# The modulation products of the second layer as VectorE multiply-adds into PSUM, TensorE summing over partitions

## Chip, cores and metric

The kernel runs on one core of a Trainium2 chip. The metric is device time of one execution, in microseconds (us), lower being better. Before the change the median of three runs was 3017.8 us (3013.01 to 3021.67).

## The reference

The reference is a two-layer diffusion backbone on 1024 latent tokens and 256 context tokens, width 1024. Layer 0 mixes tokens by retention and gated linear attention, layer 1 by windowed attention; each layer ends with a squared-ReLU MLP of width 4096. Every sub-layer is modulated by six vectors that come from one product per layer with a vector `c` (for latent tokens) or `c_ctx` (for context tokens). That product is what the change concerns:

```python
def modulation(cvec, w, b):
    m = jax.nn.silu(cvec) @ w + b          # (1024,) @ (1024, 6144) + (6144,)
    return jnp.split(m[..., None, :], 6, axis=-1)

sh1, sc1, g1, sh2, sc2, g2 = modulation(c, w_mod[i], b_mod[i])
csh1, csc1, cg1, csh2, csc2, cg2 = modulation(c_ctx, w_mod[i], b_mod[i])
h = x * (1.0 + sc1) + sh1
x = sublayer_residual(x, y, g1, ...)       # layer_norm(alpha * x + gate * y)
x = sublayer_residual(x, sq_relu_mlp(x * (1.0 + sc2) + sh2, mlp_w1[i], mlp_w2[i]), g2, ...)
```

In layer 1, the last one, the context tokens end after the keys and values of the attention, so that of the `c_ctx` vectors only `csh1` and `csc1` are used there. `w_mod[1]` is 1024 x 6144 in fp32, 24 MB. Nothing in layer 1 reads its modulation before the MLP of layer 0 is done.

## The kernel before

Activations lie with the channel on the partitions: a tile `acc` of [128, 8, N] holds 1024 channels of N tokens. There are three chunks of tokens, `CH`: chunk 0 (the context, N = 256) and chunks 1 and 2 (N = 512 each). Every product with a weight is done in three matmuls, high part by high, high by low and low by high (`mm3`, lines 200, 201, 202), since fp32r rounds. `wsplit` (lines 183 to 190) loads 128 x 1024 of a weight (line 185, SyncE's queue), rounds it on ScalarE (line 188) and makes the rest on GpSimd (line 189).

The change acts in the MLP of layer 0 (`mlp(0, ...)`). It runs over 16 blocks `b` of 256 hidden channels, and in each over the chunks 0, 1, 2; in the first and last block the chunks of 512 are cut in two halves, so that all steps there have N = 256. A step does `up` (2 x 8 x 3 matmuls into the PSUM banks 2 and 3), then ScalarE and VectorE square the result and split it (lines 981 to 985), and then `down` of the step before (8 output groups `m` of 6 matmuls each, into a ring of the four banks 0, 1, 4, 5). VectorE adds each group to `acc` (line 999), which frees its bank. So the order on TensorE is up of step n, down of step n-1, up of step n+1, and so on.

The modulation of layer 1 is worked off inside this MLP, by a generator `fill` that is advanced three times per step: after `up`, after group `m` = 3 and after group `m` = 7 of `down`. The generator is `mod_steps(1, s, mp, 1, 512)` for s = 0, 1, 2. Each advance consumes one tile `raw` of 128 x 512 of `w_mod[1]` (one of 96, one buffer, loaded at line 111 on SyncE's queue) with four matmuls (line 114): `cs`, which is SiLU of the two vectors in columns 0 and 1 and zeros up to 32, is the stationary operand, and each quarter of `raw` streams through another group of 32 columns of the array, so that the results of four quarters stand on four groups of 32 partitions of PSUM bank 7. An fp32 matmul is two records in the trace. After 32 loads `mt` is copied to SBUF by ScalarE (line 117), turned by four transposes (line 120), and VectorE adds the bias and writes `mod`, `osc` and `gta` (lines 127 to 133).

A scheduler orders each engine's instructions when the program is built; at run time every engine takes its own in that order. SyncE's queue (SP) carries the loads of the MLP's weights and of `raw`, in one order.

Of the kernel before, what the change touches and what calls it, by code (L numbers as in the profile page):

```python
# [34 lines left out]
def backbone(ctx: ExitStack, tc: tile.TileContext, xT, cin, wmod, bmod, lng, lnb, w1, w2,  # L35
# [9 lines left out]
    V, S, G, TE, SY = nc.vector, nc.scalar, nc.gpsimd, nc.tensor, nc.sync  # L45

    cp = ctx.enter_context(pool(name="cp", bufs=1))
    cp.tile([P, 16], F32, tag="pad", name="pad")
    edge = ctx.enter_context(pool(name="edge", bufs=1, side="right"))
    edge.tile([P, 120], F32, tag="edge", name="edge")  # L50
    rawp = ctx.enter_context(pool(name="rawp", bufs=3))
# [5 lines left out]
    def nm(s):  # L57
        uid[0] += 1
        return f"{s}_{uid[0]}"
# [27 lines left out]
    G.memset(ones_d, 1.0 / 1024.0)  # L87
    ones_1 = const([32], "ones_1")
    G.memset(ones_1, 1.0 / 32.0)
    ones_h = const([32], "ones_h")  # L90
    G.memset(ones_h, 1.0 / 128.0)
    eps_t = const([1], "eps_t")
# [9 lines left out]
    def mod_steps(l, s, mdp, nb=1, w=1024, tags=("raw",), bank=None):  # L102

        pM_ = bank or pM
        pt = pM_()
        n_ = 0
        for o in range(0, 2048, w):
            for k in range(KT):
                raw = mdp.tile([P, w], F32, tag=tags[n_ % len(tags)], name=nm("raw"), bufs=nb)
                n_ += 1  # L110
                SY.dma_start(raw, wmod[l, k * P:(k + 1) * P, s * 2048 + o:s * 2048 + o + w])
                yield
                for g in range(4):
                    TE.matmul(pt[32 * g:32 * g + 32, o // 4:(o + w) // 4], lhsT=cs[:, k, :],
                              rhs=raw[:, g * w // 4:(g + 1) * w // 4], start=(k == 0), stop=(k == KT - 1))
        mt = mdp.tile([P, w], F32, tag=tags[0], name=nm("mt"), bufs=nb)[:, 0:512]
        S.copy(mt, pt)
        p2 = pM_()
        for q in range(4):
            TE.transpose(p2[:, q * P:(q + 1) * P], mt[:, q * P:(q + 1) * P], ident)  # L120
        vw = "p (q g i) -> p g q i" if w == 1024 else "p (q g i) -> p q g i"
        fw = "p (g q) -> p g q" if w == 1024 else "p (q g) -> p q g"
        pv = p2.rearrange(vw, q=4, g=4)
        for si in range(2):
            idx = 2 * s + si
            sub = pv[:, :, 2 * si:2 * si + 2, 0:2] if w == 1024 else pv[:, 2 * si:2 * si + 2, :, 0:2]
            V.tensor_tensor(
                mod[:, l, idx, :, :].rearrange(fw.replace(") ->", ") j ->") + " j", g=4), sub,
                bm[:, l, idx, :].rearrange(fw, g=4)[:, :, :, None].to_broadcast(list(sub.shape)), ALU.add)
            if idx in (1, 4):  # L130
                V.tensor_scalar(osc[:, l, idx // 3], mod[:, l, idx], 1.0, None, op0=ALU.add)
            if idx in (2, 5):
                V.tensor_scalar(gta[:, l, idx // 3], mod[:, l, idx], 1.0 / ALPHA, None, op0=ALU.mult)
        yield

    def mod_chunks(l, s, bank):

# [926 lines left out]
    with pool(name="m0", bufs=1) as mp:  # L1064
        ln_ = layer_norm_steps(accs[2][:, :, 256:512], 0, 0, mp, "ln_s", "ln_q", 1, True, pL, 512)
        early = Early([new_h(hp, 1, 0, hp, (0,), (V, V)) + new_h(hp, 1, 0, hp, (256,)) + new_h(hp, 2, 0, hp, (0,)), [(None, ln_)] + new_h(hp, 2, 0, hp, (256,))], ((2, 2), (2, 2)))
        early.need(1, 0)
        adv(ln_, 1)
        hn = {}

        ticks0, ticks1 = (4, 1), (3, 2)
        norms, hgens = [], []

        def tick(k, to_free=False):
            k, kh = k
            while norms and (k > 0 or to_free):
                r_ = next(norms[0][0], "end")
                if r_ == "end":
                    hgens.append(norms.pop(0)[1])
                k -= 1  # L1080
                if k <= 0 and r_ in ("end", "free"):
                    break
            while hgens and kh > 0:
                if next(hgens[0], "end") == "end":
                    hgens.pop(0)
                else:
                    kh -= 1

        def post(ci, o0, n):
            norms.append((post_norm(accs[ci][:, :, o0:o0 + n]), post_h(ci, o0, n)))  # L1090

        def post_norm(acc):
            yield from layer_norm_steps(acc, 0, 1, (rawp, hp), "raw", "hf", 1, True, pL, 512)

        def post_h(ci, o0, n):
            sl = slice(o0, o0 + n)
            if ci > 0:
                SY.dma_start(xd[ci][:, :, sl], accs[ci][:, :, sl])
            if stop == "x2":
                SY.dma_start(dbg[:, :, CH[ci][0] + o0:CH[ci][0] + o0 + n], accs[ci][:, :, sl])  # L1100
            if o0 == 0:
                hn[ci] = h_tiles(hp, ci)
            yield from h_steps(accs[ci][:, :, sl], 1, 0, cj(ci), hn[ci][0][:, :, sl], hn[ci][1][:, :, sl], hp, "hf", 2, S)

        rest = mlp(0, [0, 1, 2], hs, accs, wg, mp, post, chain(*[mod_steps(1, s_, mp, 1, 512) for s_ in range(3)]), tick, ticks0, early)
        tick((1, 0), True)
        hs = hn

# [415 lines left out]
```

## Time and profile before

| | us |
|---|---|
| median of three runs | 3017.8 (3013.01 to 3021.67) |
| the profiled execution's own time | 3027.1 |
| its span, first to last instruction | 3025.3 |
| TensorE busy in the span | 2922.6 (97%) |
| VectorE busy | 1525.4 (50%) |
| ScalarE busy | 976.4 (32%) |
| GpSimd busy | 809.9 (27%) |

Durations below are of the one profiled execution, which took 9.3 us more than the median of the runs. Of its 3027.1 us, 1.8 lie outside the span. PE is TensorE, PEld its weight loads, DVE is VectorE, ACT ScalarE, POOL GpSimd, SP SyncE. Matmuls are pipelined: a record is longer than the time by which it moves the next one back, so what a matmul costs is read from start to start, not from its length.

### The profile page before, as it was taken

The numbers are of one execution on the slowest core, as the hardware profiler recorded it, in microseconds if no ns is written. First come the engines' busy times: TensorE is split into PE (matmuls) and PEld (weight loads), VectorE is DVE, ScalarE is ACT, GpSimd is POOL, SyncE is SP. The second block draws the span as 40 slices with busy tenths as digits, with TensorE's granted clock in tenths as the row PEclk, the third lists the DMA queues.
The fourth block names the chain that finished last, engine by engine and source line by source line (L and its number), as shares of the span: only waits on it lengthen the run. The fifth ranks groups of instructions, "written<-read, shape, count | busy, mean of one in ns | idle before, by whom it ended". The sixth has DMA issues, their size and how long they took to land. (4 is left out here: it accounts for less than half of the span.)

```text
span 3025.3 us, 43318 instructions
## 1 busy us (share of the span) xinstructions
PE 2922.6 (97%) x17856; PEld 2386.6 (79%) x17856; DVE 1525.4 (50%) x2489; ACT 976.4 (32%) x1617; POOL 809.9 (27%) x609
## 2 busy tenths in 40 slices
PE   7989998999999999999999999999999999999997
PEld 4766788888888888888888777677678888888886
DVE  3654477777434333433334654666775333333445
ACT  4534344444211111111111442556653221112113
POOL 3120145445211111111111342244344221122121
PEclk9999999999999999999999999999999999999999
DMA  7278575663222222221100166222221111111111
GB/s 254 96 229 254 185 260 193 202 202 112 78 70 79 68 80 67 80 67 49 42 29 15 67 200 179 75 79 74 71 70 63 56 56 36 49 56 50 36 41 56
DMA packets 164261, 304.52 MB, mean 101 GB/s; under 512 B 13504, under 2 KB 90560, under 8 KB 163552
## 3 DMA queue, kind: packets, MB, share of 16 engines
q1 hardware_dynamic: 145648, 272.91, 28.0%
q0 software_dynamic: 6480, 16.26, 1.9%
q10 hardware_dynamic: 11936, 12.59, 1.4%
q8 instruction: 140, 2.29, 0.3%
q14 instruction: 57, 0.47, 0.0%
HBM read 257.67 MB, written 44.04 MB: 100 GB/s over the span
## 5 line engine op out<-in xcount | busy, mean ns | idle before, releaser
L189 POOL TENSOR_TENSOR w<-raw,w 128x1024 fp32r<-128x1024 f32 x210 | 507.4, 2424 | 1683.4 <-ACT w L188 1642.9
L999 DVE SCALAR_TENSOR_TENSOR acc<-k,gta,acc 128x512 f32<-128x512 f32 (+1 forms) x704 | 443.2, 648 | 831.0 <-PE k L202 823.7
L200 PE MATMUL k<-hh,w 128*128 128x256 f32 (+1 forms) x1632 | 556.9, 342 | 5.1 <-DVE hh L196 3.4
L201 PE MATMUL k<-hl,w 128*128 128x256 f32 (+1 forms) x1632 | 555.0, 340 | 4.0 <-POOL hl L197 3.4
L202 PE MATMUL k<-hh,w 128*128 128x256 f32 (+1 forms) x1632 | 551.1, 338 | 0.2 <-POOL w L189 0.2
L188 ACT CAST w<-raw 128x1024 fp32r<-128x1024 f32 x260 | 269.5, 1048 | 822.5 <-PE k L202 540.3
L200 PE MATMUL k<-uh,w 128*128 128x512 f32 (+1 forms) x1408 | 503.0, 357 | 4.2 <-DVE acc L999 4.0
L201 PE MATMUL k<-ul,w 128*128 128x512 f32 (+1 forms) x1408 | 495.4, 352 | 0.0
L202 PE MATMUL k<-uh,w 128*128 128x512 f32 (+1 forms) x1408 | 494.8, 351 | 0.0
L200 PEld LDWEIGHTS k<-hh,w 128*128 128x128 f32 x1632 | 312.5, 192 | 54.9 <-issue 16.3
L201 PEld LDWEIGHTS k<-hl,w 128*128 128x128 f32 x1632 | 312.5, 192 | 44.8 <-issue 7.6
L202 PEld LDWEIGHTS k<-hh,w 128*128 128x128 f32 x1632 | 312.4, 191 | 34.4 <-issue 2.8
L200 PEld LDWEIGHTS k<-uh,w 128*128 128x128 f32 x1408 | 266.5, 189 | 55.4 <-issue 14.2
L981 ACT ACTIVATE r<-k 128x512 f32<-128x512 f32 (+1 forms) x176 | 90.9, 516 | 649.7 <-PE k L202 649.0
L202 PEld LDWEIGHTS k<-uh,w 128*128 128x128 f32 x1408 | 266.7, 189 | 36.7 <-issue 1.0
L201 PEld LDWEIGHTS k<-ul,w 128*128 128x128 f32 x1408 | 266.7, 189 | 35.3 <-issue 0.8
L200 PE MATMUL k<-yh,w 128*128 128x256 f32 (+1 forms) x544 | 183.9, 338 | 10.1 <-DVE acc L693 10.1
L201 PE MATMUL k<-yl,w 128*128 128x256 f32 (+1 forms) x544 | 181.2, 333 | 0.0
L202 PE MATMUL k<-yh,w 128*128 128x256 f32 (+1 forms) x544 | 181.1, 333 | 0.0
L984 DVE TENSOR_TENSOR r<-r 128x1024 f32<-128x1024 f32 (+1 forms) x88 | 113.9, 1295 | 127.7 <-ACT uh L983 127.4
L673 POOL TENSOR_SCALAR acc<-acc,lg_t,lb_t 128x256 f32<-128x256 f32 x124 | 103.1, 847 | 116.1 <-DVE acc L667 46.8
L200 PEld LDWEIGHTS k<-yh,w 128*128 128x128 f32 x544 | 106.5, 196 | 22.6 <-DVE acc L693 11.5
(300 smaller groups left out, 4419.2 us busy)
## 6 DMA issues: line engine op xcount, KB each, us to landing
raw<-in_w SPq DMA_DIRECT2D x128, 512.0 KB, 3.4
raw<-in_wo SPq DMA_DIRECT2D x72, 512.0 KB, 3.5
raw<-in_wmod SPq DMA_DIRECT2D x128, 256.0 KB, 2.7
raw<-in_wfm SPq DMA_DIRECT2D x48, 512.0 KB, 5.6
raw<-in_wmod SPq DMA_DIRECT2D x32, 512.0 KB, 4.2
kt<-kd SPq DMA_DIRECT2D x20, 512.0 KB, 6.0
qt<-qT POOLq DMA_DIRECT2D x32, 256.0 KB, 4.3
qT<-qT ACTq DMA_DIRECT2D x30, 256.0 KB, 3.7
```

Of the source, the lines that this page charges most:

```text
L188: S.copy(hi, raw)
L189: (eng or G).tensor_tensor(lo, raw, hi.bitcast(F32), ALU.subtract)
L200: TE.matmul(pt, lhsT=wh, rhs=xh, start=start, stop=False)
L201: TE.matmul(pt, lhsT=wh, rhs=xl, start=False, stop=False)
L202: TE.matmul(pt, lhsT=wl, rhs=xh, start=False, stop=stop)
L673: G.tensor_scalar(acc[:, k, :], acc[:, k, :], lg_t[:, l, s, k:k + 1], lb_t[:, l, s, k:k + 1], op0=ALU.mult, op1=ALU.add)
L981: S.activation(rf[:, i, :n], pts[i][:, :n], AF.Relu)
L984: V.tensor_tensor(rf[:, :, :n], rf[:, :, :n], rf[:, :, :n], ALU.mult)
L999: V.scalar_tensor_tensor(a_, pt[:, :n], gta[:, l, 1, m, cj(ci):cj(ci) + 1], a_, op0=ALU.mult, op1=ALU.add)
```

## The change

The three calls of `mod_steps` for layer 1 are replaced by three of a new generator, `mod_sums`. It loads the same 96 times 256 KB of `w_mod[1]` into one buffer `raw`. The multiplications by SiLU of the vectors, and the sum over the eight blocks of 128 input channels, are now VectorE's: for the first block `pt = raw * cs[:, 0, j]`, for the others `pt = raw * cs[:, k, j] + pt`, with `pt` in PSUM bank 7. What is left of the sum, over the 128 partitions, is done by TensorE: `pt` is copied to SBUF by ScalarE and each 128 columns of it are the stationary operand of a matmul whose moving operand is one column of ones, `one_c`. The result is one column per 128 output channels, on the partitions where `mod` needs it, so there are no transposes.

For s = 0 (`sh1` and `sc1`) both vectors are needed: there the tile holds two blocks of 256 columns, and each load is followed by four VectorE instructions on 128 x 256. For s = 1 and 2 only the latent vector is computed, one instruction on 128 x 512 per load. In all there are 128 + 64 such instructions, 16 copies instead of 3, and 16 x 4 matmuls with one moving column in place of 384 matmuls with 128 and 12 transposes. The generator has 128 steps, before it had 99. The padding of the constants' pool is cut from 16 to 8 columns.

```diff
@@ -45,7 +45,7 @@
     V, S, G, TE, SY = nc.vector, nc.scalar, nc.gpsimd, nc.tensor, nc.sync
 
     cp = ctx.enter_context(pool(name="cp", bufs=1))
-    cp.tile([P, 16], F32, tag="pad", name="pad")
+    cp.tile([P, 8], F32, tag="pad", name="pad")
     edge = ctx.enter_context(pool(name="edge", bufs=1, side="right"))
     edge.tile([P, 120], F32, tag="edge", name="edge")
     rawp = ctx.enter_context(pool(name="rawp", bufs=3))
@@ -87,6 +87,8 @@
     G.memset(ones_d, 1.0 / 1024.0)
     ones_1 = const([32], "ones_1")
     G.memset(ones_1, 1.0 / 32.0)
+    one_c = const([1], "one_c")
+    G.memset(one_c, 1.0)
     ones_h = const([32], "ones_h")
     G.memset(ones_h, 1.0 / 128.0)
     eps_t = const([1], "eps_t")
@@ -132,6 +134,45 @@
             if idx in (2, 5):
                 V.tensor_scalar(gta[:, l, idx // 3], mod[:, l, idx], 1.0 / ALPHA, None, op0=ALU.mult)
         yield
+
+    def mod_sums(l, s, mdp, bank):
+
+
+        nj = 2 if s == 0 else 1
+        w = 512 // nj
+        nb = w // P
+        for o in range(0, 2048, w):
+            pt = bank()
+            for k in range(0, KT, nj):
+                raw = mdp.tile([P, 512], F32, tag="raw", name=nm("raw"), bufs=1)
+                SY.dma_start(raw.rearrange("p (a c) -> p a c", a=nj),
+                             wmod[l, k * P:(k + nj) * P, s * 2048 + o:s * 2048 + o + w]
+                             .rearrange("(a p) c -> p a c", p=P))
+                yield
+                for a in range(nj):
+                    src = raw[:, a * w:(a + 1) * w]
+                    for j in range(nj):
+                        dst = pt[:, j * w:(j + 1) * w]
+                        if k + a == 0:
+                            V.tensor_scalar(dst, src, cs[:, 0, j:j + 1], None, op0=ALU.mult)
+                        else:
+                            V.scalar_tensor_tensor(dst, src, cs[:, k + a, j:j + 1], dst, op0=ALU.mult, op1=ALU.add)
+            mt = mdp.tile([P, 512], F32, tag="raw", name=nm("mt"), bufs=1)
+            S.copy(mt, pt)
+            yield
+            p2 = bank()
+            for b in range(4):
+                TE.matmul(p2[:, b:b + 1], lhsT=mt[:, b * P:(b + 1) * P], rhs=one_c, start=True, stop=True)
+            idx = 2 * s + o // 1024
+            ks = slice(o % 1024 // P, o % 1024 // P + nb)
+            for j in range(nj):
+                V.tensor_tensor(mod[:, l, idx, ks, j], p2[:, j * nb:(j + 1) * nb], bm[:, l, idx, ks], ALU.add)
+                if idx in (1, 4):
+                    V.tensor_scalar(osc[:, l, idx // 3, ks, j], mod[:, l, idx, ks, j], 1.0, None, op0=ALU.add)
+                if idx in (2, 5):
+                    V.tensor_scalar(gta[:, l, idx // 3, ks, j], mod[:, l, idx, ks, j], 1.0 / ALPHA, None,
+                                    op0=ALU.mult)
+            yield
 
     def mod_chunks(l, s, bank):
 
@@ -1102,7 +1143,7 @@
                 hn[ci] = h_tiles(hp, ci)
             yield from h_steps(accs[ci][:, :, sl], 1, 0, cj(ci), hn[ci][0][:, :, sl], hn[ci][1][:, :, sl], hp, "hf", 2, S)
 
-        rest = mlp(0, [0, 1, 2], hs, accs, wg, mp, post, chain(*[mod_steps(1, s_, mp, 1, 512) for s_ in range(3)]), tick, ticks0, early)
+        rest = mlp(0, [0, 1, 2], hs, accs, wg, mp, post, chain(*[mod_sums(1, s_, mp, pM) for s_ in range(3)]), tick, ticks0, early)
         tick((1, 0), True)
         hs = hn
```

VectorE, in the first third of the stage, a `down` of chunk 0 with N = 256 (`acc_370` is chunk 0's accumulator, L999 before and L1040 after is the addition that frees a bank, L984/L985 and L1025/L1026 are the squaring and splitting of the step before). Before:

```order
L999 SCALAR_TENSOR_TENSOR acc_370_2834<-k_1050_7769,gta,acc_370_2834 128x256
L984 TENSOR_TENSOR r_7755<-r_7755 128x1024
L999 SCALAR_TENSOR_TENSOR acc_370_2834<-k_1051_7777,gta,acc_370_2834 128x256
L985 TENSOR_TENSOR ul_7756<-r_7755,uh_7759 128x1024
L999 SCALAR_TENSOR_TENSOR acc_370_2834<-k_1052_7785,gta,acc_370_2834 128x256
L999 SCALAR_TENSOR_TENSOR acc_370_2834<-k_1053_7793,gta,acc_370_2834 128x256
L999 SCALAR_TENSOR_TENSOR acc_370_2834<-k_1055_7807,gta,acc_370_2834 128x256
```

The same place after, with the two loads whose products come just ahead of it:

```order
L159 SCALAR_TENSOR_TENSOR k_1020_7539<-raw_7625,cs,k_1020_7539 128x256 x4
L159 SCALAR_TENSOR_TENSOR k_1020_7539<-raw_7662,cs,k_1020_7539 128x256 x4
L1040 SCALAR_TENSOR_TENSOR acc_370_2836<-k_1052_7767,gta,acc_370_2836 128x256
L1040 SCALAR_TENSOR_TENSOR acc_370_2836<-k_1053_7775,gta,acc_370_2836 128x256
L1025 TENSOR_TENSOR r_7753<-r_7753 128x1024
L159 SCALAR_TENSOR_TENSOR k_1020_7539<-raw_7700,cs,k_1020_7539 128x256
L1026 TENSOR_TENSOR ul_7754<-r_7753,uh_7757 128x1024
L159 SCALAR_TENSOR_TENSOR k_1020_7539<-raw_7700,cs,k_1020_7539 128x256
L1040 SCALAR_TENSOR_TENSOR acc_370_2836<-k_1054_7783,gta,acc_370_2836 128x256
L159 SCALAR_TENSOR_TENSOR k_1020_7539<-raw_7700,cs,k_1020_7539 128x256
L1040 SCALAR_TENSOR_TENSOR acc_370_2836<-k_1055_7791,gta,acc_370_2836 128x256
L159 SCALAR_TENSOR_TENSOR k_1020_7539<-raw_7700,cs,k_1020_7539 128x256
```

Four multiply-adds on 128 x 256 stand between the additions of this `down`, and eight ahead of it, each four of which need their own load of the one buffer.

VectorE, later, between a `down` of chunk 0 and the next of chunk 1, while TensorE does an `up`. Before, with nothing of the modulation there:

```order
L999 SCALAR_TENSOR_TENSOR acc_370_2834<-k_1171_8708,gta,acc_370_2834 128x256
L999 SCALAR_TENSOR_TENSOR acc_370_2834<-k_1172_8716,gta,acc_370_2834 128x256
L999 SCALAR_TENSOR_TENSOR acc_371_2836<-k_1180_8794,gta,acc_371_2836 128x512
L984 TENSOR_TENSOR r_8780<-r_8780 128x1024
L999 SCALAR_TENSOR_TENSOR acc_371_2836<-k_1181_8802,gta,acc_371_2836 128x512
```

After, a like place:

```order
L1040 SCALAR_TENSOR_TENSOR acc_370_2836<-k_1517_11228,gta,acc_370_2836 128x256
L1040 SCALAR_TENSOR_TENSOR acc_370_2836<-k_1518_11236,gta,acc_370_2836 128x256
L159 SCALAR_TENSOR_TENSOR k_1508_11174<-raw_11306,cs,k_1508_11174 128x512
L159 SCALAR_TENSOR_TENSOR k_1508_11174<-raw_11340,cs,k_1508_11174 128x512
L159 SCALAR_TENSOR_TENSOR k_1508_11174<-raw_11375,cs,k_1508_11174 128x512
L159 SCALAR_TENSOR_TENSOR k_1508_11174<-raw_11457,cs,k_1508_11174 128x512
L1040 SCALAR_TENSOR_TENSOR acc_371_2838<-k_1526_11308,gta,acc_371_2838 128x512
L1025 TENSOR_TENSOR r_11297<-r_11297 128x1024
```

Four multiply-adds with four loads stand in a row, ahead of the additions of the next `down`.

TensorE, between a `down` and an `up`. Before, the four matmuls of one load:

```order
L201 MATMUL k_1494_11221<-ul_10986,w_10270 128x512
L202 MATMUL k_1494_11221<-uh_10989,w_10270 128x512
L114 MATMUL k_1358_10191<-raw_11194,cs 32x128 x4
L200 MATMUL k_1496_11235<-hh_6751,w_10695 128x512
L201 MATMUL k_1496_11235<-hl_6752,w_10695 128x512
```

After, between two groups of a `down`, the four matmuls that sum one `mt` over its partitions:

```order
L242 MATMUL k_1096_8089<-ul_7892,w_6906 128x512
L243 MATMUL k_1096_8089<-uh_7895,w_6906 128x512
L165 MATMUL k_1097_8096<-one_c,mt_8063 128x1 x4
L241 MATMUL k_1098_8104<-uh_7895,w_6901 128x512
L242 MATMUL k_1098_8104<-ul_7892,w_6901 128x512
```

There are 96 places of the first kind before, and 16 of the second after.

## Rows read from the trace of the kernel before

**Rows 1.** Busy time of each engine in four stretches (stretch, its length, then busy us and, in brackets, instructions of PE, PEld, DVE, ACT and POOL; granted clock; share of the DMA engines; GB/s). The MLP of layer 0 runs from about 741 to 1640 us.

```profile
740.00:760.00 20.00, 19.56 (x148) 15.89 (x147) 18.15 (x29) 13.71 (x29) 13.17 (x11) 1.00 0.18 58
760.00:780.00 20.00, 19.87 (x176) 18.08 (x176) 16.10 (x28) 8.05 (x16) 11.74 (x12) 1.00 0.23 66
...
900.00:1000.00 100.00, 100.00 (x589) 80.78 (x588) 38.16 (x53) 17.15 (x24) 14.41 (x7) 1.00 0.22 67
741.00:1640.00 899.00, 895.09 (x5351) 744.87 (x5351) 353.57 (x516) 167.93 (x241) 163.01 (x81) 1.00 0.20 62
```

**Rows 2.** TensorE in order of time between an `up` and a `down` with N = 512 (start us, length us, engine, line, operation, tiles, shapes).

```profile
907.84 0.39 PE L202 MATMUL k<-hh,w 128*128 128x512 f32 x1
...
908.52 0.39 PE L202 MATMUL k<-hh,w 128*128 128x512 f32 x1
908.84 0.43 PE L114 MATMUL k<-raw,cs 128*32 128x128 f32 x8
909.20 0.50 PE L200 MATMUL k<-uh,w 128*128 128x512 f32 x1
909.53 0.39 PE L201 MATMUL k<-ul,w 128*128 128x512 f32 x1
```

**Rows 3.** The same in a `down` with N = 256.

```profile
953.68 0.28 PE L201 MATMUL k<-ul,w 128*128 128x256 f32 x1
953.80 0.28 PE L202 MATMUL k<-uh,w 128*128 128x256 f32 x1
954.01 0.43 PE L114 MATMUL k<-raw,cs 128*32 128x128 f32 x8
954.37 0.38 PE L200 MATMUL k<-uh,w 128*128 128x256 f32 x1
954.59 0.28 PE L201 MATMUL k<-ul,w 128*128 128x256 f32 x1
```

**Rows 4.** Groups of instructions on TensorE from 741 to 1640 us, shapes kept apart (line, engine, operation, tiles, shapes, count | busy us, mean ns | idle us just before them, and what ended it).

```profile
L114 PE MATMUL k<-raw,cs 128*32 128x128 f32 x768 | 41.3, 285 | 3.3 <-DMA raw<-in_wmod 3.3
...
L120 PE MATMUL k<-ident,mt 128*128 128x128 f32 x12 | 1.8, 273 | 0.0
```

**Rows 5.** TensorE around the transposes of one `mt`.

```profile
934.39 0.39 PE L200 MATMUL k<-uh,w 128*128 128x512 f32 x1
934.62 0.60 PE L120 MATMUL k<-ident,mt 128*128 128x128 f32 x4
934.97 0.47 PE L201 MATMUL k<-ul,w 128*128 128x512 f32 x1
935.28 0.39 PE L202 MATMUL k<-uh,w 128*128 128x512 f32 x1
```

**Rows 6.** TensorE in the scans of layer 0: two fp32 matmuls (four records) with 128 x 128 stationary and 64 moving columns.

```profile
396.81 0.56 PE L904 MATMUL k<-qt,S 128*128 128x64 f32 x4
397.21 0.44 PE L902 MATMUL k<-Pg,vt 128*128 128x128 f32 x2
```

**Rows 7.** Groups of instructions on VectorE from 750 to 1700 us, shapes kept apart, columns as in rows 4.

```profile
L999 DVE SCALAR_TENSOR_TENSOR acc<-k,gta,acc 128x512 f32<-128x512 f32 x224 | 165.5, 747 | 250.8 <-PE k L202 250.3
L999 DVE SCALAR_TENSOR_TENSOR acc<-k,gta,acc 128x256 f32<-128x256 f32 x182 | 82.1, 478 | 190.8 <-PE k L202 190.4
...
L649 DVE TENSOR_TENSOR acc<-acc,k 128x512 f32<-128x512 f32 x11 | 7.1, 676 | 0.0
```

**Rows 8.** VectorE in a `down` of chunk 0 (N = 256), in order of time; the last column is idle time and what ended it.

```profile
951.96 0.48 DVE L999 SCALAR_TENSOR_TENSOR acc<-k,gta,acc 128x256 f32<-128x256 f32 x1 [11.39 <-PE k L202]
952.41 1.23 DVE L984 TENSOR_TENSOR r<-r 128x1024 f32<-128x1024 f32 x1
953.56 0.48 DVE L999 SCALAR_TENSOR_TENSOR acc<-k,gta,acc 128x256 f32<-128x256 f32 x1
953.95 1.21 DVE L985 TENSOR_TENSOR ul<-r,uh 128x1024 fp32r<-128x1024 f32 x1
955.08 1.65 DVE L999 SCALAR_TENSOR_TENSOR acc<-k,gta,acc 128x256 f32<-128x256 f32 x4
957.05 0.48 DVE L999 SCALAR_TENSOR_TENSOR acc<-k,gta,acc 128x256 f32<-128x256 f32 x1 [0.32 <-PE k L202]
957.77 0.48 DVE L999 SCALAR_TENSOR_TENSOR acc<-k,gta,acc 128x256 f32<-128x256 f32 x1 [0.23 <-PE k L202]
```

**Rows 9.** The loads of `raw` at line 111 (those of layer 0 among them).

```profile
L111 SPq DMA_DIRECT2D raw<-in_wmod x112: 327/328/797, 185.6 to 1372.5; - x112
...
DMA to landing us min/median/max: 2.4/2.6/6.2
```

**Rows 10.** The loads at line 142, of two blocks of 128 x 512 of `w_mod[0]` in one (512 KB).

```profile
L142 SPq DMA_DIRECT2D raw<-in_wmod x16: 378/378/384, 395.7 to 656.8; - x16
...
DMA to landing us min/median/max: 3.5/4.1/6.7
```

**Rows 11.** VectorE in the first block of the MLP, the longest idle time before 785 us.

```profile
784.49 0.69 DVE L984 TENSOR_TENSOR r<-r 128x512 f32<-128x512 f32 x1 [5.46 <-ACT uh L983]
```

**Rows 12.** ScalarE's copies of `mt` before (four in all, one of them in layer 0).

```profile
L117 ACT COPY mt<-k x4: 586/590/591, 285.5 to 1377.0; 128x512 f32<-128x512 f32 x4
```

## Prediction

> **What bounds the kernel now.** I looked first at the busy times by stretch [rows 1], because the change touches one stage alone, the MLP of layer 0. There TensorE is busy for 895.09 of 899 us at a granted clock of 1.00 (the upper of its two levels, 2.4 GHz), and VectorE for 353.57, some 39%. A busy TensorE may still wait inside its records, so I looked next at what VectorE waits for [rows 7]: nearly all its idle time ahead of the additions of line 999 (250.3 of 250.8 us, 190.4 of 190.8) ended with a matmul. TensorE sets the pace, VectorE follows. So time taken off TensorE in this stage comes off the end, until VectorE is late. The reader should see one exception in the same view: from 740 to 780 us VectorE is busy for 18.15 and 16.10 of 20 us [rows 1], since the layer norms and splits of the first chunks lie there.
>
> **What is removed.** A matmul's cost is read from start to start. With N = 512 the starts are 0.227 us apart (907.84 to 908.52 for three). Around the eight records of one load it is 908.52 to 909.53 for two steps, 1.01 us; less 2 x 0.227 that is 0.556 us [rows 2]. With N = 256 the starts are 0.12 apart, and two steps with a load between take 953.80 to 954.59, 0.79 us; less 0.24 that is 0.55 [rows 3]. The two agree, though the matmuls around them differ by a factor of two, so I take 0.553 for each load. There are 768 records [rows 4], so 96 loads: 96 x 0.553 = 53.1 us. The three times four transposes cost 934.39 to 935.28 less 2 x 0.227, 0.44 us each [rows 5], 1.3 us together. TensorE also waited 3.3 us for loads of `raw` [rows 4]; VectorE will wait for them in its place. Removed in all: 57.7 us.
>
> **What is added on TensorE.** Sixteen times four fp32 matmuls, eight records, with 128 x 128 stationary and one moving column. No row has one moving column. The nearest has the same stationary shape and 64 columns: four records from 396.81 to 397.21, 0.10 us each [rows 6], so 0.80 us for eight and 12.8 us for sixteen. From above the transposes bound it, 0.11 per record [rows 5]: 14.1 us. From below the eight records with 32 stationary columns do, 0.55 [rows 2, 3]: 8.8 us. I take 12.8, by the row with the same stationary operand. A gain is excluded, since these matmuls replace nothing that is not counted already. Net on TensorE: 57.7 - 12.8 = 44.9 us.
>
> **What is added on VectorE.** On 128 x 256, multiply-adds that follow each other start 0.39 us apart (four in 1.65 us, one 0.48) [rows 8]; 128 of them are 50 us. On 128 x 512 the addition of line 999 has a mean of 0.747 and line 649 one of 0.676 [rows 7]; at 0.7, 64 are 45 us. None of these rows writes to PSUM, which the new ones do; I assume that costs no more than the spread between the two. VectorE comes to about 354 + 95 of some 860 us, 52%. Over the stage this lies beside TensorE's work. Where it doesn't:
>
> First block. VectorE had 5.75 us idle in the 40 us from 740 to 780 [rows 1]. The products of four loads come into it, 16 x 0.39 = 6.2 us, and TensorE, without some six loads' matmuls, wants to be through 3.3 us earlier. So VectorE has 34.25 + 6.2 = 40.5 us of work in 36.7, and some two more go on waiting for the first loads: about 6 us late. The idle 5.46 us after that [rows 11] is cover for a part. I take 6, with 0 and 12 as ends.
>
> `down` with N = 256 in later blocks. Groups end 0.72 us apart there; the last starts at 957.05, so the seventh at 956.33. It needs the bank whose addition is the first of four from 955.08, done at 955.56 [rows 8]: 0.77 us to spare. Of that, 0.55 goes since the load's matmuls inside this `down` [rows 3] are gone; 0.22 is left. By the order two multiply-adds stand ahead of that addition in the worst such `down`, 0.78 us: 0.6 us of waiting. There are four or five such places in the part with s = 0 and a little in the ten later ones: 3.5 us, ends 0 and 10.
>
> The loads. VectorE must now wait for each `raw`, with one buffer: product, issue, landing 2.6 us after [rows 9], product. In the place where four stand in a row, that is 4 x 0.7 + 3 x (2.6 + 0.3), 11.5 us. TensorE's `up` beside it takes 48 x 0.227 = 10.9, and the first group of the next `down` another 1.4, so 12.3 us pass before an addition is due, and three more banks are free then. Covered, narrowly; I take 0 and price the other case below. With s = 0 a load has twice as many and shorter runs; the nearest rows are 2.6 us [rows 9] and, for twice the bytes, 4.1 [rows 10]; eight products with one load between take 3.1 + 3 to 4.4 us, less than 10.9.
>
> The sums. TensorE takes its instructions in order, so it stops at the matmul with `mt` if ScalarE's copy, 0.59 us [rows 12], is not done. The order puts most of the sixteen well behind the copy. At nothing to one copy each that is 0 to 9.4 us; I take the middle, 4.7. SyncE's queue carries weights behind these loads; TensorE, idle for 4 of 899 us [rows 1] of which 3.3 are for `raw` [rows 4], was never short of weights, so nothing for that.
>
> **The sum.** 44.9 - 6 - 3.5 - 4.7 = 30.7, say 31 us. The profiled execution would go from 3027.1 to 2996. It was 9.3 us above the median, so against that it is 3017.8 - 31 = **2987 us**. With every unknown at its good end: 57.7 - 8.8 = 48.9, 2969 us. At the bad ends: 57.7 - 14.1 - 31.4 = 12.2, 3006 us.
>
> **Rivals.** First, the other side: the loads hold VectorE up. Everything on VectorE stands behind a product that waits for its `raw`, additions that free banks included, and then TensorE stops. A wait that shows costs up to a landing, 2.6 us [rows 9], and the 44.9 us are gone after 17 of them. That it happens is helped by the single buffer and by weight loads between in SyncE's queue; 24 of 96 (each fourth, the one that comes last in a row of four) would be 62 us, giving 3017.8 - 44.9 + 62 = 3035 us. Against it: four banks, and VectorE's idle time ahead of the additions [rows 7]. In this rival the Trainium skill sides: "PSUM — Partial Sum Buffer", section "Engine vs sequencer instructions", has VectorE's queue as strictly first in, first out. By that rule no addition passes a waiting product; the trace agrees as far as it goes, since VectorE's instructions of rows 8 ran in the program's order.
>
> Second, VectorE becomes the bound while s = 0 lasts: all the bad ends together, 3006 us. The first block's VectorE load [rows 1] speaks for it, the idle time behind it against.
>
> Third, the matmuls cost less than their gap. Eight records are on the engine for 0.43 us, one alone for a mean of 0.285 [rows 3, 4], so they start within 0.145 us. If only that comes back and the rest of the gap stays with the change from `up` to `down`, the gain is 96 x 0.145 = 13.9 + 1.3 + 3.3 - 12.8 = 5.7, and less 14.2 of waits it is 8.5 us slower: 3026 us. Rows 3 speak against it: the gap is the same inside a `down`, where nothing else changes. The Trainium skill, "TensorE: Matmul & The Clock Gate", section "Measured speedup vs the span model", says that matmuls on different column groups overlap and add some 4 ns each. By that rule four with 128 columns cost little more than one; the trace has 0.55 us for them with the gaps on both sides, and that measurement decides.
>
> Fourth, the change does not take the time off the end: what follows the MLP waits for something else, and the kernel stays at 3018 us. Little speaks for it, since TensorE is 97% busy over the span.
>
> **How the numbers follow.** Forecast 0.70, first rival 0.10, second 0.13, third 0.03, fourth 0.04. The forecast's own range is 2969 to 3006. To hold 8 in 10 the range goes from 2967 to 3016; the first and third rivals and half the fourth stay outside, with a little below. A measurement here can tell some 0.3%, 9 us, from nothing. Faster: forecast and second rival, less a little of the latter's edge, 0.82. Same: that edge and the fourth, 0.06. Slower: the first and third, less rounding, 0.12.
>
> **What would show it.** Right: in windows such as 900 to 1000 TensorE stays at 100% with more of the MLP's matmuls in it; starts around an advance are 0.227 apart; the MLP ends some 30 us sooner. The sums read 0.8 us from start to start. Right on VectorE: about 95 us of multiply-adds, and idle time that still ends with matmuls. Wrong: idle time on VectorE that ends with a load of `raw`, followed by TensorE waiting for additions (first rival); such waits in the first block alone (second); a start-to-start gap left at the advances (third); TensorE waiting for ScalarE's `mt` by more than 5 us in all (my term for the sums).

## The result and the profile after

The changed kernel takes 2991.37 us (median of four runs, 2990.12 to 2999.63) against 3018.64 of the kernel before on the same chip: a ratio of 0.9918, 95% interval 0.9894 to 0.9941. On a second chip it was 2990.58 against 3024.68, ratio 0.9898 (0.9880 to 0.9917). So it is 0.8 to 1.0% faster, some 27 to 34 us. The profiled execution took 2999.63 us, its span is 2997.8 us.

First the busy times by stretch, columns as in [rows 1]. The stretch that ended near 1640 us before now ends near 1610; the last `down`s of the MLP stand behind it, among layer norms, up to 1683 us (before, up to 1713).

```profile
740.00:760.00 20.00, 19.16 (x145) 16.30 (x139) 18.87 (x31) 14.31 (x30) 15.40 (x11) 1.00 0.21 66
760.00:780.00 20.00, 18.61 (x142) 16.77 (x141) 16.54 (x30) 8.59 (x19) 8.36 (x8) 1.00 0.13 41
...
900.00:1000.00 100.00, 100.00 (x526) 86.02 (x525) 57.27 (x107) 18.59 (x26) 17.26 (x8) 1.00 0.23 72
741.00:1610.00 869.00, 861.56 (x4713) 746.19 (x4713) 448.43 (x737) 176.72 (x258) 165.99 (x81) 1.00 0.21 65
```

TensorE is still busy nearly throughout, at a granted clock of 1.00, and the stage is shorter. VectorE has gone from 353.57 us [rows 1] to 448.43, now 52% of the stage. In the first 40 us TensorE is idle for 2.23 us where it was for 0.57.

The groups of the same stage, columns as in [rows 4]:

```profile
L1040 DVE SCALAR_TENSOR_TENSOR acc<-k,gta,acc 128x512 f32<-128x512 f32 x224 | 164.1, 746 | 106.1 <-PE k L243 105.9
...
L241 PE MATMUL k<-uh,w 128*128 128x256 f32 x304 | 88.2, 290 | 5.2 <-DVE acc L1040 4.8
...
L1040 DVE SCALAR_TENSOR_TENSOR acc<-k,gta,acc 128x256 f32<-128x256 f32 x152 | 67.9, 477 | 63.7 <-PE k L243 62.7 <-POOL w L230 0.7
...
L159 DVE SCALAR_TENSOR_TENSOR k<-raw,cs,k 128x256 f32<-128x256 f32 x112 | 54.4, 486 | 41.6 <-DMA raw<-in_wmod 39.6
L159 DVE SCALAR_TENSOR_TENSOR k<-raw,cs,k 128x512 f32<-128x512 f32 x56 | 42.1, 753 | 119.8 <-DMA raw<-in_wmod 119.7
...
L165 PE MATMUL k<-one_c,mt 128*128 128x1 f32 x128 | 15.3, 240 | 0.0
...
L161 ACT COPY mt<-k 128x512 f32<-128x512 f32 x16 | 9.4, 587 | 60.4 <-DVE k L159 60.4
```

The idle time ahead of the additions still ends with matmuls, but it is 169.8 us where it was 441.6 (in the somewhat longer stretch of [rows 7]), and 159.3 us have a new owner: the multiply-adds of line 159 wait for `raw`. TensorE's own line 241 has a new releaser, VectorE's additions. This is what the prediction named as the sign of its first rival; the question is what it costs.

A place where it costs something, VectorE in order of time, in the part with N = 512 loads (columns as in [rows 8]):

```profile
1158.73 0.74 DVE L1040 SCALAR_TENSOR_TENSOR acc<-k,gta,acc 128x512 f32<-128x512 f32 x1
1161.55 0.76 DVE L159 SCALAR_TENSOR_TENSOR k<-raw,cs,k 128x512 f32<-128x512 f32 x1 [2.07 <-DMA raw<-in_wmod]
1168.01 0.75 DVE L159 SCALAR_TENSOR_TENSOR k<-raw,cs,k 128x512 f32<-128x512 f32 x1 [5.70 <-DMA raw<-in_wmod]
1171.50 0.75 DVE L159 SCALAR_TENSOR_TENSOR k<-raw,cs,k 128x512 f32<-128x512 f32 x1 [2.73 <-DMA raw<-in_wmod]
1172.16 0.87 DVE L1040 SCALAR_TENSOR_TENSOR acc<-k,gta,acc 128x256 f32<-128x256 f32 x2
```

SyncE's DMA queue at that time (start, length of all in the row, line, tile, count):

```profile
1158.85 0.33 SPq L148 DMA_DIRECT2D raw<-in_wmod  x1
1160.87 2.68 SPq L226 DMA_DIRECT2D raw<-in_w  x2
1163.64 8.97 SPq L148 DMA_DIRECT2D raw<-in_wmod  x3
```

And TensorE, where the next `down` starts:

```profile
1171.39 0.28 PE L243 MATMUL k<-uh,w 128*128 128x256 f32 x1
1172.70 0.39 PE L241 MATMUL k<-uh,w 128*128 128x256 f32 x1 [1.03 <-DVE acc L1040]
```

Read them together. The product at 1161.55 frees the single buffer at 1162.3; two loads of weights stand ahead in SyncE's queue, so the next `raw` is issued at 1163.64 and its product starts at 1168.01. From product to product it is 6.46 us, where the prediction's chain had 0.7 + 2.9 = 3.6. The additions of 1172.16 stand behind the last product in VectorE's queue, and TensorE, through with its banks, starts 1.31 us after the matmul before instead of 0.12.

The sum over partitions, TensorE in order of time (columns as in [rows 2]):

```profile
907.44 0.39 PE L243 MATMUL k<-uh,w 128*128 128x512 f32 x1
907.67 0.95 PE L165 MATMUL k<-one_c,mt 128*128 128x1 f32 x8
908.48 0.49 PE L241 MATMUL k<-uh,w 128*128 128x512 f32 x1
908.80 0.40 PE L242 MATMUL k<-ul,w 128*128 128x512 f32 x1
```

From 907.44 to 908.80 it is 1.36 us; less 2 x 0.227 that is 0.906 us for one sum, not 0.80.

To compare kernels, I summed TensorE's start-to-start times from 735 to 1610 us over the pace of [rows 2, 3] (0.227 or 0.120 us each) and sorted the excess: next to a matmul of the modulation (up to the successor of the full matmul behind it); in the first block (735 to 800 us) elsewhere; after 800 us elsewhere. The stage's length is from the first to the last `uh` matmul of layer 0. This is worked out from all records, in us, and good to some half a microsecond:

| kernel | modulation | first block | after 800 us | stage |
|---|---|---|---|---|
| before | 58.3 | 3.8 | 1.0 | 961.5 |
| after | 14.7 | 6.8 | 9.8 | 929.4 |
| after, second chip | 14.6 | 7.6 | 8.1 | 926.3 |
| before, an eighth of its matmuls | 8.0 | 8.4 | 1.6 | 913.1 |
| 16 of 96 loads | 14.4 | 8.8 | 0.1 | 918.5 |
| generator not advanced in the first block | 14.4 | 8.8 | 7.9 | 926.1 |
| two buffers | 14.7 | 6.6 | 11.2 | 928.2 |
| three buffers | 14.6 | 7.6 | 2.5 | 920.8 |
| three buffers, ScalarE's queue | 14.8 | 7.8 | 2.2 | 920.7 |
| s = 0 as before | 28.9 | 4.0 | 5.7 | 935.4 |
| three buffers, ScalarE's queue, third chip | 14.8 | 7.7 | 1.8 | 920.4 |
| the same, not advanced in the first block | 14.4 | 6.9 | 1.4 | 919.7 |
| the same, one matmul of four per sum | 3.6 | 7.6 | 2.7 | 910.3 |
| the same, twice the multiply-adds | 14.6 | 7.9 | 3.3 | 924.5 |

The stage became 32.1 us shorter: 43.6 less of modulation, 3.0 more in the first block, 8.8 more behind it, 31.8 together. The whole profiled execution became 27.5 us shorter, since it reaches the stage 2.5 us later (754.0 us for 751.5) and spends 2.1 more behind it (1314.4 for 1312.3). On the second chip the stage starts at 740.9 us and 1312.9 follow it, so these differences are those of single executions.

### The profile page after: what moved, and what is told of

Read it like the earlier page. It is cut to its first block, busy times and chain, and to the rows that moved or that the text cites. A ratio compares the mean times of both kernels' runs of the same rounds, so it can differ in the third digit from the quotient of the medians.

```text
span 2997.8 us, 42313 instructions
## 1 busy us (share of the span) xinstructions
PE 2886.7 (96%) x17204; PEld 2389.1 (80%) x17204; DVE 1618.5 (54%) x2709; ACT 982.1 (33%) x1630; POOL 811.2 (27%) x610
## 5 line engine op out<-in xcount | busy, mean ns | idle before, releaser
L1040 DVE SCALAR_TENSOR_TENSOR acc<-k,gta,acc 128x512 f32<-128x512 f32 (+1 forms) x704 | 441.2, 648 | 567.4 <-PE k L243 559.9
L159 DVE SCALAR_TENSOR_TENSOR k<-raw,cs,k 128x256 f32<-128x256 f32 (+1 forms) x168 | 96.5, 575 | 161.4 <-DMA raw<-in_wmod 159.3
L1025 DVE TENSOR_TENSOR r<-r 128x1024 f32<-128x1024 f32 (+1 forms) x88 | 110.0, 1250 | 68.9 <-ACT uh L1024 68.8
```

The source lines that it names most:

```text
L159: V.scalar_tensor_tensor(dst, src, cs[:, k + a, j:j + 1], dst, op0=ALU.mult, op1=ALU.add)
L1025: V.tensor_tensor(rf[:, :, :n], rf[:, :, :n], rf[:, :, :n], ALU.mult)
L1040: V.scalar_tensor_tensor(a_, pt[:, :n], gta[:, l, 1, m, cj(ci):cj(ci) + 1], a_, op0=ALU.mult, op1=ALU.add)
```

## The experiments

**Is a load's 0.55 us on TensorE's path?** The kernel before, with an eighth of its modulation matmuls.

```diff
                 yield
+                if l == 1 and k > 0:
+                    continue
                 for g in range(4):
...
-                              start=(k == 0), stop=(k == KT - 1))
+                              start=(k == 0), stop=(l == 1 or k == KT - 1))
```

> The kernel before, but of the eight matmul groups of each 128 x 512 result of the second layer's modulation only the first is made: 12 loads of 96 keep their four matmuls, the other 84 are loaded and not used, so that seven eighths of that product are left out. My theory: a load's matmuls cost 0.553 us from start to start, all of it on the path, so 84 x 0.553 = 46 us go: 2972 us. Rival (only the 0.145 us within which the eight records start come back): 84 x 0.145 = 12 us, 3006 us. Should the pace be set elsewhere, nothing goes: 3018 us.

Measured: 2976.0 us against 3023.18, ratio 0.9845 (0.9826 to 0.9864), 47 us less; my theory had 46. 84 groups of matmuls are gone, so each is worth 47.2 / 84 = 0.56 us; the interval allows 0.49 to 0.63. The parts agree with the table: 50.3 us less next to the modulation, of which 3.3 were waits for `raw`, and 4.6 more in the first block. The prediction's third rival, 0.145 for each, falls.

**Do the loads or the products hold TensorE?** The changed kernel with 16 of its 96 loads; the products reuse what was loaded, so the rest of `w_mod` is left out.

```diff
-                raw = mdp.tile([P, 512], F32, tag="raw", name=nm("raw"), bufs=1)
-                SY.dma_start(raw.rearrange("p (a c) -> p a c", a=nj),
...
+                if k == 0:
+                    raw = mdp.tile([P, 512], F32, tag="raw", name=nm("raw"), bufs=1)
+                    SY.dma_start(raw.rearrange("p (a c) -> p a c", a=nj),
...
```

> The changed kernel with one load for each PSUM result: 16 loads of 96 are kept, and all multiply-adds of a result read that one tile, so that most of the weights are left out of the product; VectorE's instructions are as many and as long. My theory: what TensorE still waits for in the later blocks (6.7 us after 1040 us, some 2 us between 800 and 1040) comes from products that wait for their load with additions queued behind, so 6 to 9 us go: 2983 to 2985 us, and VectorE's idle time that ends with a load falls from 170 us to under 40. Rival: it is VectorE's added work itself that makes additions late: 2991 us, with the same waits of TensorE.

Measured: 2981.3 us, ratio 0.9868 (0.9848 to 0.9888). Of VectorE's waits from 741 to 1610 us, those for matmuls and for loads (waiter, releaser, sum in us, times, longest):

```profile
DVE acc L1041 <- PE k L244: 291.7, 143, 11.3
DVE k L158 <- DMA raw<-in_wmod: 9.8, 7, 3.1
```

and after 800 us TensorE's excess is 0.1 us, with every product still made. The waits there come from the loads, the multiply-adds themselves cost nothing that shows; that holds for the N = 256 `down`s too, for which the prediction took 3.5 us. Fewer loads also leave SyncE's queue to the weights; the trials with more buffers below keep all 96.

**One buffer or two?** The tiles `raw` and `mt` take turns over two buffers from the sixteenth on.

```diff
+    n_raw = [0]
+
+    def raw_tag():
+        n_raw[0] += 1
+        ts = ('raw', 'ln_q') if n_raw[0] > 15 else ("raw",)
+        return ts[n_raw[0] % len(ts)]
...
-                raw = mdp.tile([P, 512], F32, tag="raw", name=nm("raw"), bufs=1)
+                raw = mdp.tile([P, 512], F32, tag=raw_tag(), name=nm("raw"), bufs=1)
...
-            mt = mdp.tile([P, 512], F32, tag="raw", name=nm("mt"), bufs=1)
+            mt = mdp.tile([P, 512], F32, tag=raw_tag(), name=nm("mt"), bufs=1)
```

> The changed kernel with a second buffer for the loads (from the 16th tile on, in space that the first layer norm has left), so that a load lands while the product before it runs. My theory: the waits after 800 us shrink from 8.7 to 2 or 3 us: 2985 us. Rival (VectorE's work itself): 2991 us. A third: the scheduler, which now sees loads in time, sets six or seven products in a row where there were four, and a landing shows again: 2988 to 2993 us with the waits in other places.

Measured: 2993.6 us, ratio 0.9905 (0.9886 to 0.9923): no gain that shows. VectorE's wait for `raw` is halved, 80.0 us for 169.9 (with one buffer first, then with two):

```profile
DVE k L159 <- DMA raw<-in_wmod: 159.3, 54, 8.6
...
DVE k L157 <- DMA raw<-in_wmod: 10.6, 10, 2.5
```

```profile
DVE k L166 <- DMA raw<-in_wmod: 77.5, 44, 6.5
...
DVE k L164 <- DMA raw<-in_wmod: 2.5, 2, 2.2
```

But TensorE's excess does not fall, it is 11.2. The order now brings up to seven products in a row, where with one buffer it was four, and a landing still lies before the last of them. Here five stand in a row from 1216.73 us on, and these are the last three:

```profile
1225.98 1.55 DVE L166 SCALAR_TENSOR_TENSOR k<-raw,cs,k 128x512 f32<-128x512 f32 x2 [6.48 <-DMA raw<-in_wmod]
1229.86 0.75 DVE L166 SCALAR_TENSOR_TENSOR k<-raw,cs,k 128x512 f32<-128x512 f32 x1 [2.33 <-DMA raw<-in_wmod]
1230.52 0.87 DVE L1047 SCALAR_TENSOR_TENSOR acc<-k,gta,acc 128x256 f32<-128x256 f32 x2
```

Two loads of weights, from 1218.92 to 1221.59 us in SyncE's queue, stand ahead of these loads too.

**The first block.** The generator is not advanced there, all of its work is asked for one block later.

```diff
-                if m in (3, 7):
+                if m in (3, 7) and b > 0:
...
-            adv(fill, 1)
+            if b > 0:
+                adv(fill, 1)
```

> The changed kernel, but the generator is not advanced in the MLP's first block, where VectorE has the layer norms and splits. My theory: the 3.0 us of new waits between 735 and 800 us go and nothing comes back, since the 129 advances that are needed fit in the 139 that are left: 2988 us. Rival: the same waits come in the second block, whose products are the ones of the first now, since four short multiply-adds per load are what costs: 2991 us.

Measured: 2989.6 us, ratio 0.9891 (0.9873 to 0.9909). The edit took the sums out of the first block, but not all products: the scheduler set the next block's ahead, and 16 ran between 735 and 800 us, for 24 and 31 in the two executions of the changed kernel. Only two of them stood before the longest wait there, which ends with an addition that is behind a split of the layer norm's result and a squaring in VectorE's order:

```profile
771.38 0.39 PE L241 MATMUL k<-uh,w 128*128 128x256 f32 x1 [2.12 <-DVE acc L1040]
```

The first block's excess is no smaller, 8.8 us, and with the old matmuls cut to an eighth, where VectorE has no products at all, it is 8.4. Taken over the same work (from 15 us before the stage's first `uh` matmul to 46 us behind it) it is 6.6 us in both executions of the changed kernel, with 24 products, 7.5 here with 12, and 7.1 with none. So it isn't the products: TensorE, without the matmuls that stood there, comes sooner to layer norms and splits that are not ready.

**The changed kernel again**, as the measure on the second chip.

> The changed kernel again, as the measure for the three others on this chip. Some 27 us below the kernel before (ratio 0.991). In its trace TensorE's extra waits from 800 us to the end of layer 0's MLP should again come to some 8 to 10 us and stand behind additions that wait behind a product that waits for its load; if they stand in quite other places or are gone, they are scatter of one execution and no property of the order.

Measured: 2990.58 us, ratio 0.9898. TensorE's largest waits stood at the same places, 0.7 to 1.3 us each: they end at 766, 822, 1160 and 1218 us for 779, 834, 1173 and 1231, since this execution is some 13 us earlier there. The first ends with a split on GpSimd, the three after 800 us with VectorE's additions. They are the order's, not scatter.

**Who would bound s = 0?** A third of the products goes back to TensorE.

```diff
-        rest = mlp(0, [0, 1, 2], hs, accs, wg, mp, post, chain(*[mod_sums(1, s_, mp, pM) for s_ in range(3)]), tick, ticks0, early)
+        rest = mlp(0, [0, 1, 2], hs, accs, wg, mp, post, chain(mod_steps(1, 0, mp, 1, 512), *[mod_sums(1, s_, mp, pM) for s_ in (1, 2)]), tick, ticks0, early)
```

> The third of the modulation with s = 0 is made as before (32 loads, eight fp32 matmuls of TensorE each), the two other thirds as after. My theory: TensorE bounds the stage, so the kernel gets 32 x 0.553 = 17.7 us of matmuls back and one round of transposes, 0.4, and loses eight sums, 8 x 0.9 = 7.2; of the waits from 800 to 1040 us (2.4) nothing is left, in the first block little changes. Together some 8 us slower than the changed kernel, and about 19 faster than the kernel before. Rival (VectorE is the bound while s = 0 lasts): taking 64 us of multiply-adds off VectorE there brings more than TensorE loses, so that this is faster than the changed kernel, by up to 10 us. In the trace, the first theory has TensorE's waits from 735 to 800 us as in the changed kernel (some 8 with the layer norms' own); the rival has them go.

Measured: 3001.46 us, ratio 0.9925 (0.9907 to 0.9944), 10.9 us above the changed kernel. The rival had it faster: it falls. One sign of mine was wrong: the first block's excess did go, to 4.0 us, and 5.3 us of matmuls came back there, while VectorE has no products. With the matmuls cut to an eighth it has none either, and the excess is 8.4; so it is TensorE's matmuls that make the waits go, not VectorE's relief.

**Three buffers.** The same edit with three tags in the tuple, `('raw', 'ln_q', 'ln_s')`.

> The loads' tile takes turns over three buffers from the sixteenth load on; nothing else. If the single buffer causes VectorE's waits for loads, then with three these fall from 170 us to under 30, and TensorE's waits from 800 to 1610 us (8 to 10 us) to under 3: 6 us faster than the changed kernel. If it is the place in SyncE's queue (behind weight loads that wait for buffers of their own), VectorE's idle time ahead of the products stays above 60 us as with two buffers, and the time within 3 us of the changed kernel's. Third: the scheduler now puts more products in a row, and waits of TensorE for additions come behind VectorE's work in place of its waiting; time within 3 us too, but with VectorE's idle time for loads small.

Measured: 2983.87 us, ratio 0.9866 (0.9845 to 0.9886), 6.7 us below the changed kernel on that chip. The two intervals overlap a little; the excess after 800 us, 2.5 where it was 8.1, is the clearer sign. VectorE's wait at the products is 36.4 us, though up to eight now stand in a row:

```profile
DVE k L166 <- DMA raw<-in_wmod: 36.4, 27, 5.8
```

**Three buffers and another queue.**

```diff
-                SY.dma_start(raw.rearrange("p (a c) -> p a c", a=nj),
+                S.dma_start(raw.rearrange("p (a c) -> p a c", a=nj),
```

> Three buffers, and the loads are issued on ScalarE's queue in place of SyncE's, so that no weight load stands ahead of them. If SyncE's queue is what delays them, the idle time of VectorE ahead of its products falls well under that with three buffers alone, and TensorE's waits from 800 to 1610 us go to under 3: some 6 us faster than the changed kernel. Against it: ScalarE now waits where a buffer isn't free yet, and its copies of uh, and of the weights' high parts stand behind that; if that decides, TensorE waits for ScalarE's copies and the kernel is slower than the changed one by several us. If the waits on TensorE come from products in a row and not from loads, no difference over 3 us.

Measured: 2981.82 us, ratio 0.9862 (0.9845 to 0.9878), 8.8 us below the changed kernel. VectorE's waits:

```profile
DVE acc L1047 <- PE k L250: 279.7, 155, 11.3
...
DVE k L166 <- DMA raw<-in_wmod: 29.4, 25, 3.4
```

To three buffers alone (36.4 us of waiting, 2983.87) no difference can be told, so with three buffers the queue doesn't matter; whether it would with one or two wasn't tried. On a third chip, as the measure for the next three:

> The kernel with three buffers and the loads on ScalarE's queue again, as the measure for the other three on this chip: ratio 0.986 to the kernel before, some 42 us. TensorE's waits from 800 us to the end of the stage some 2 us.

Measured: 2984.25 us, ratio 0.9867 (0.9846 to 0.9888).

**The same, not advanced in the first block.** The edits of both.

> The kernel with three buffers and ScalarE's queue; besides, no load, product or sum in the MLP's first block, the work moves one block on. If the products in the first block make TensorE wait there (as my prediction had it, 6 us), its waits from 735 to 800 us go from 8 to 3 and the time falls by 5. If these waits are those of the layer norms and splits, which TensorE now reaches 3 us sooner since the modulation's matmuls there are gone, they stay at 7 to 9 us and the time within 3 us.

Measured: 2984.38 us, ratio 0.9857 (0.9834 to 0.9881): no difference, first block 6.9 us. Here too 16 products ran there, for 28 before, so it shows that fewer products bring nothing.

**The price of the sums.**

```diff
-            for b in range(4):
+            V.memset(p2[:, 0:4], 0.0)
+            for b in range(1):
```

> The kernel with three buffers and ScalarE's queue; of the four matmuls of each of the sixteen sums only the first is made, so it leaves out three quarters of the modulation's sums (the columns are set to zero in their place). A sum takes 0.90 us from start to start, so TensorE should give 16 x 0.675 = 10.8 us back, and the kernel be 11 us faster. Rival: the matmuls overlap with others, so that a record's 0.11 us is not a price, and the time stays within 3 us.

Measured: 2972.96 us, ratio 0.9832 (0.9807 to 0.9856), 11.3 us less; modulation's excess is 3.6 us for 14.8. One of the four, TensorE in order of time:

```profile
894.95 0.39 PE L251 MATMUL k<-uh,w 128*128 128x512 f32 x1
895.18 0.28 PE L173 MATMUL k<-one_c,mt 128*128 128x1 f32 x2
895.32 0.48 PE L249 MATMUL k<-uh,w 128*128 128x512 f32 x1
895.63 0.40 PE L250 MATMUL k<-ul,w 128*128 128x512 f32 x1
```

895.63 - 894.95 - 2 x 0.227 = 0.226 us, a quarter of 0.906: four cost four times one.

**Twice the multiply-adds.**

```diff
+    pad = cp.tile([P, 8], F32, tag="pad", name="pad")
+    G.memset(pad, 0.0)
...
                             V.scalar_tensor_tensor(dst, src, cs[:, k + a, j:j + 1], dst, op0=ALU.mult, op1=ALU.add)
+                            V.scalar_tensor_tensor(dst, src, pad[:, 0:1], dst, op0=ALU.mult, op1=ALU.add)
```

> The kernel with three buffers and ScalarE's queue; behind each multiply-add stands a second one of the same size that multiplies by zero, so VectorE gets some 97 us more work in the stage and nothing else changes. If VectorE has room (TensorE bounds the stage, and additions lie within the banks' cover), the time is 0 to 6 us up. If VectorE is near its limit at the N = 256 downs, where two multiply-adds ahead of an addition left some 0.2 us, each of some thirty such places costs 0.4 to 0.8 us more: 12 to 24 us slower.

Measured: 2985.38 us, ratio 0.9875 (0.9853 to 0.9897), 1.1 us above its measure, though VectorE's busy time from 741 to 1600 us is 540.01 us:

```profile
741.00:1600.00 859.00, 854.45 (x4700) 741.60 (x4694) 540.01 (x901) 177.39 (x258) 168.40 (x82) 1.00 0.21 66
```

against 446.82 of the kernel with three buffers and ScalarE's queue on the second chip:

```profile
741.00:1600.00 859.00, 854.50 (x4687) 743.07 (x4687) 446.82 (x726) 170.10 (x245) 159.03 (x75) 1.00 0.20 64
```

The stage is 4.1 us longer, 924.5 for 920.4, and 2.8 of that lies behind the last product, where the two executions of the changed kernel also differ by 2.7. VectorE has room.

## Why the prediction was right, point by point

**What bounds the stage: right.** TensorE. 93 us more of VectorE cost nothing that can be told from scatter; 84 groups of matmuls less gave 47 us; a third of the matmuls back cost 11. So the second rival falls, and the fourth with the first measurement, whose interval ends at 0.9941.

**Removed, 57.7 us: right.** The excess next to the modulation was 58.3 us, and the trial with an eighth of the matmuls prices a load at 0.56 us for the 0.553 of the working. The Trainium skill, "TensorE: Matmul & The Clock Gate", section "Measured speedup vs the span model", has matmuls on different column groups add some 4 ns each. Inside a load's group the trace of the kernel before agrees in size: the records of the four column groups start 7 ns apart, and all eight within 0.15 us. The other 0.4 of the 0.56 us stand at the group's two ends (0.09 us before it, 0.20 and 0.11 behind it, from the records of [rows 2]), and the trial shows that they come back too.

**The sums, 12.8 us: mis-sized.** They took 14.6, by 0.906 each. From the first of the eight records to the matmul behind them it is 0.81 us (907.67 to 908.48), as the working had it with 0.80. What it left out is the end of the gap: the matmul behind starts its successor 0.32 us later in place of 0.227. The four records of [rows 6] were read without that step, the loads of [rows 2] and, in what is removed, the transposes of [rows 5] with it. The upper end, 14.1, was a little low for the same reason. The net is 43.6 us for 44.9.

**VectorE's 95 us: right.** Its busy time rose from 353.57 us [rows 1] to 448.43, by 94.9. Back to back the products, with PSUM as input and output, start some 0.40 us apart with 128 x 256 and 0.67 with 128 x 512. Their records are longer, 486 and 753 ns (110.2 us in all), since each overlaps the next, as the additions' of line 999 do with 478 and 747 [rows 7]. The assumption that PSUM costs no more than the spread between the two rows held.

**First block, 6 us: half, and for another reason.** The excess rose by 3.0 and 3.8 us. The working added 6.2 us of products to VectorE's 34.25 and took 3.3 from TensorE. Only the second part was right: with no products there (the matmuls cut to an eighth) the excess is 8.4, with some of them moved on it is 8.8 with one buffer and 6.9 with three, with twice the multiply-adds 7.9, and with the matmuls back 4.0.

**N = 256 `down`s, 3.5 us: wrong.** Without the loads' waits after 800 us 0.1 us is left, with all products made. Two multiply-adds ahead of the addition do not reach the banks' cover; with twice as many the excess after 800 us is 3.3 us against 1.8.

**The loads, 0: wrong, and the largest miss.** The step "covered, narrowly" fails at the time from product to product. It took 2.6 + 0.3 us for issue and landing, the median of [rows 9], whose longest landing is 6.2. By the records of the trace that holds in 58 of 80 rounds (the buffer's release, the issue, the next product), those without a weight load between: 0.03 us to the issue and 2.8 from there to the product, medians. In the eight with two weight loads ahead it was 1.3 us, at most 4.3, to the issue and 4.2 to the product; the place shown has 1.3 and 4.4. TensorE's excess after 800 us rose by 7.1 to 8.8 us, and falls to 2.5 with three buffers and to 0.1 with 16 of the loads. The first rival's mechanism is there, at 8 us and not at 62: most of VectorE's 170 us of waiting costs TensorE nothing. The rule of the Trainium skill that the prediction cited for it ("PSUM — Partial Sum Buffer", "Engine vs sequencer instructions"), VectorE's queue as strictly first in, first out, agrees with the additions of 1172.16, which stood behind a product that waited.

**TensorE waiting for `mt`, 4.7 us: wrong.** It waited 0.2 us in all. The order gave the copy time at all but one of the sixteen.

So the four waits, 14.2 us by the working, came to some 12 (3.0 + 8.8 + 0.2): nearly the predicted sum from other terms, and that is luck: the three terms that it had were 11 us too large, and the loads, put at nothing, cost 8.8. 2987 us was 4 us low, less than the first measurement's interval.

**The best version.** Three buffers with the loads on ScalarE's queue: 2981.82 and 2984.25 us on two chips, 0.986 to 0.987 of the kernel before.

## What to carry to other kernels

Small matmuls between full ones cost TensorE their whole gap from start to start; read it there, and not from their length. Work moved to an engine with idle time is free only if what it waits for is: an in-order engine that now waits for a single-buffered load holds everything behind it, so price a round (release, place in the DMA queue, landing under load) and not a landing alone. Here three buffers took most of that wait away, and two did not. That two fell short because the order then put more products in a row is read from places like the one shown and was not tested by itself; with three there were as many in a row.

## What the runs showed of the hardware

An fp32 matmul with 128 x 128 stationary and one moving column costs 0.226 us from start to start between full matmuls, in a group of four as by itself. Each is two records, and inside a group of four they start 0.11 us apart, as the transposes with 128 moving columns do [rows 5].

Executions of the same kernel differ by 20 us (2981.85 to 3002.07 for the changed one), and part of it lies ahead of the stage, where nothing changed: its first `uh` matmul is at 754.0 us in one profile and at 740.9 in the other, with a granted clock from 300 to 400 us of 0.94 and 0.97:

```profile
300.00:400.00 100.00, 90.45 (x577) 79.33 (x576) 47.79 (x102) 40.85 (x70) 22.25 (x23) 0.94 0.64 201
```

```profile
300.00:400.00 100.00, 91.50 (x621) 79.84 (x620) 51.16 (x110) 40.10 (x66) 24.75 (x25) 0.97 0.65 206
```

(the first is of the profile above, the second of the one on the second chip). Whether the clock makes all of that is not shown. From there to the last `uh` matmul of the stage the two differ by 3.1 us. A stage's own length tells small changes better than the whole.
